# Where an attention kernel divides by its softmax sums: each tile of exponentials on GpSimd, or four query tiles' outputs at once through a float32 product

## The chip, the cores and the metric

The kernel runs on one core of one Trainium2 chip. The metric is the device time of one execution in microseconds (us). A core has a matrix engine (TensorE, PE in the profile; PEld are its weight loads), VectorE (DVE), ScalarE (ACT), GpSimd (POOL) and SyncE (SP), which issues nearly all of this kernel's DMAs. Each engine runs its own queue of instructions in order and waits on semaphores of the others. The kernel uses PSUM, where PE writes its results, as eight banks of 128 x 512 float32.

## The reference, cut to what matters

The model is a two-layer diffusion transformer block on 1024 latent tokens and 256 context tokens, with width 1024. In each layer a modulated norm is followed by a projection and three token mixers side by side (neighbourhood attention, a gated linear scan, a short convolution), an output projection, and a mixture of 16 experts. The change is in the neighbourhood attention. For each of six heads of 64 channels, a query sees 8 rows x 16 columns of latent keys around it, and all 256 context keys:

```python
s_loc = einsum('bjqhd,bjkhd->bhjqk', q_r, k_loc) * scale + bias
s_loc = where(win_mask, s_loc, -inf)
s_ctx = einsum('bjqhd,bchd->bhjqc', q_r, k_ctx) * scale
p = softmax(concatenate([s_loc, s_ctx], -1), -1)
o_loc = einsum('bhjqk,bjkhd->bjqhd', p[..., :n_loc], v_loc)
o_ctx = einsum('bhjqc,bchd->bjqhd', p[..., n_loc:], v_ctx)
return o_loc + o_ctx
```

In the first layer the context tokens also attend to one another; in the second they are not needed.

## The kernel before, in words

Each layer runs norm, projection with scan and convolution, neighbourhood attention, output projection, routing and experts, in this order. The document calls the attention and the part of the output projection beside it the attention stage. It handles the six heads as three pairs (`na_pair`, L771). A pair's queries are cut into tiles of 128, and these into groups: in layer 0 a group of two context tiles, and in both layers two groups of four latent tiles. That makes nine groups in layer 0 and six in layer 1, three of the fifteen with two tiles and twelve with four.

For one tile and one head, `na_scores` (L708) takes the products of queries and keys on PE into two PSUM banks (`sA`, `sB`; the keys are split in a high and a low part, so each is a pair of products). DVE adds the bias, negates and takes the minimum over the row (L743, L745, into `S` and `mn`). ACT takes the exponential in place and sums each row into `sm` (L750). DVE inverts the sum (L751), and POOL multiplies the whole 128 x 832 (768 at the edges, 256 for context) tile by it (L752). `na_transpose` (L755) turns the tile in pieces of 128 x 128 on PE into bank stream "A" (`npt`, two banks taken in turn); ACT and DVE copy them to `PT`. Then PE multiplies them with the values into `nao`, one bank for the whole group, both heads side by side: rows are channels (head 0 in rows 0 to 63, head 1 in 64 to 127), columns are queries. At the group's end ACT copies `nao` to `mo`, and SP stores it to DRAM (`mix`), from where the output projection reads it again (`mst`, L813).

`S`, `PT` and `mo` have two buffers each. Beside the attention runs other work. While pairs 0 and 1 are computed, `na_prep` (L647) makes the next pair's queries and keys (`qn`, `nro`, `qd` on DVE and POOL, transposes `nt` on PE, `QT`, `KH`, `KL`), and `adaln` streams the modulation weights (`wm`) through PE (`aps`). Beside pair 2 runs `wout_part` (L831): the part of the output projection (`po`) that doesn't need the attention. In the tables below, stage one is pairs 0 and 1, stage two is pair 2 with `wout_part`.

The order on each engine is not that of the code: the framework's scheduler places every instruction by its own estimate of times, so a change in one place can move many others. `order` rows below are taken from the built programs.

## Time and profile before

| what | value |
|---|---|
| three timed runs | 2744.39, 2754.39, 2755.64 us, median 2754.39 |
| the profiled execution's own time | 2748.93 us |
| its span in the trace | 2747.2 us |
| stage one, layer 0 and layer 1 | 657 to 784 us, 2066 to 2190 us |
| stage two, layer 0 and layer 1 | 784 to 912 us, 2190 to 2325 us |

Busy time of an engine is the time in which it has at least one instruction running. A matmul's end is modelled, and they are pipelined, so a busy PE is not always PE at its peak. PEclk is the granted clock of TensorE as a share of its higher level (1.00 is 2.4 GHz, 0.5 is 1.2 GHz). A float32 product is two records on PE in this trace, a transpose or a product of the rounded float32 kind (`fp32r`) is one. The chain of waits follows the work that ended last back from the last instruction, and gives each step to the engine or transfer that it waited for.

### The profile page before, as it was taken

Reading aid. Unit: us, or ns where it says so; the run is one execution under the profiler, and the core shown is the slowest. Engines: PE = TensorE matmul, PEld = TensorE weight load, DVE = VectorE, ACT = ScalarE, POOL = GpSimd, SP = SyncE. Lnnn points to the kernel's source line nnn. Section 1 sums busy time; section 2 is a strip of 40 time slices with the busy share of each in tenths; the row PEclk is TensorE's granted clock in tenths of the full one; section 3 lists DMA queues with packets and bytes.
Section 4 is the critical chain, followed back from the end, with each engine's and each line's share of the span. In section 5 each row is a group of like instructions: output and inputs, shape, how many; then the busy total and the mean of one; then the engine's idle time right before and its main releaser. Section 6 shows DMA issues by size and latency. Waiting matters only on the chain.

```text
span 2747.2 us, 55415 instructions
## 1 busy us (share of the span) xinstructions
PE 2520.3 (92%) x21959; PEld 1923.8 (70%) x21959; DVE 1800.3 (66%) x3542; ACT 1132.7 (41%) x1878; POOL 1050.2 (38%) x1125
## 2 busy tenths in 40 slices
PE   7999999988999979999997999999879899589997
PEld 4988877885577855555554988778864677357664
DVE  4247776756777487777754347677767774687874
ACT  4224434324554534444433324344324454445452
POOL 1035454534544733323321035355554442222242
PEclk9999999998999979999998999999989899789999
DMA  7332324246444857888887332323176355779994
GB/s 277 104 105 71 103 72 124 64 140 209 150 141 148 302 190 261 285 271 296 262 279 231 90 109 72 114 76 103 50 208 222 100 164 185 283 269 369 378 376 129
DMA packets 347938, 507.14 MB, mean 185 GB/s; under 512 B 53380, under 2 KB 203072, under 8 KB 346592
## 3 DMA queue, kind: packets, MB, share of 16 engines
q1 hardware_dynamic: 336416, 465.85, 50.1%
q0 software_dynamic: 11264, 37.75, 5.9%
q8 instruction: 173, 2.83, 0.4%
q14 instruction: 85, 0.70, 0.1%
HBM read 410.10 MB, written 94.90 MB: 184 GB/s over the span
## 4 chain that ended last, share of the span: by engine, by line
PE 71%; DVE 15%; DMA 5%; issue 3%; ACT 2%; POOL 2%; SPq 1%; POOLq 0%; DVEq 0%; ACTq 0%
PE pj L277 15%; PE pg L1280 13%; PE pd L1335 8%; PE pj L288 8%; PE po L828 6%; PE nao L786 3%; PE npt L762 2%; PE pgc L1265 2%; DVE Kt L375 2%; PE aps L157 2%; PE hl L341 1%; PE sA L733 1%; DVE Kt L376 1%; DVE kz L355 1%; PE hl L365 1%
## 5 line engine op out<-in xcount | busy, mean ns | idle before, releaser
L1182 DVE TENSOR_TENSOR ewl<-est,ewh 128x2048 fp32r<-128x2048 f32 x126 | 298.3, 2371 | 112.6 <-ACT ewh L1178 108.1
L1178 ACT CAST ewh<-est 128x2048 fp32r<-128x2048 f32 x128 | 243.5, 1906 | 173.6 <-PE pg L1280 122.6
L277 PE MATMUL pj<-hl,whi 128*128 128x320 f32 (+2 forms) x912 | 314.2, 345 | 0.0
L277 PE MATMUL pj<-hh,whi 128*128 128x320 f32 (+2 forms) x912 | 312.5, 343 | 0.7 <-ACT pev L420 0.7
L277 PE MATMUL pj<-hh,wlo 128*128 128x320 f32 (+2 forms) x912 | 312.9, 343 | 0.0
L288 PE MATMUL pj<-whi,hh 128*128 128x256 f32 x960 | 279.8, 292 | 8.8 <-ACT nev L566 8.5
L288 PE MATMUL pj<-whi,hl 128*128 128x256 f32 x960 | 276.4, 291 | 0.9 <-DVE hl L239 0.9
L288 PE MATMUL pj<-wlo,hh 128*128 128x256 f32 x960 | 276.3, 289 | 0.0
L1335 PE MATMUL pd<-est,hidT 128*128 128x512 f32 x512 | 232.2, 596 | 2.1 <-ACT hidT L1302 2.1
L288 PEld LDWEIGHTS pj<-whi,hh 128*128 128x128 f32 x960 | 187.7, 195 | 12.0 <-ACT nev L566 9.3
L288 PEld LDWEIGHTS pj<-wlo,hh 128*128 128x128 f32 x960 | 187.5, 195 | 2.2 <-issue 1.5
L288 PEld LDWEIGHTS pj<-whi,hl 128*128 128x128 f32 x960 | 185.7, 195 | 3.8 <-DVE hl L239 1.5
L377 POOL TENSOR_TENSOR Qt<-Qt,tot 64x320 f32<-64x320 f32 x144 | 128.8, 894 | 150.9 <-PE hl L341 93.5
L277 PEld LDWEIGHTS pj<-hh,whi 128*128 128x128 f32 x912 | 174.8, 192 | 14.4 <-ACT pev L420 1.0
L277 PEld LDWEIGHTS pj<-hl,whi 128*128 128x128 f32 x912 | 174.9, 192 | 14.0 <-issue 1.2
L277 PEld LDWEIGHTS pj<-hh,wlo 128*128 128x128 f32 x912 | 175.0, 192 | 13.7 <-issue 1.4
L752 POOL TENSOR_SCALAR S<-S,sm 128x768 f32<-128x768 f32 (+2 forms) x108 | 112.7, 1045 | 186.3 <-DVE sm L751 153.2
L1335 PEld LDWEIGHTS pd<-est,hidT 128*128 128x128 f32 x512 | 95.2, 189 | 110.7 <-issue 103.3
L265 DVE TENSOR_TENSOR wlo<-wst,whi 128x1024 fp32r<-128x1024 f32 (+1 forms) x72 | 81.6, 1149 | 138.5 <-ACT whi L264 137.7
L1280 PE MATMUL pg<-ewh,xh 128*128 128x512 f32 x512 | 157.0, 425 | 2.9 <-ACT xh L1235 2.8
L1280 PE MATMUL pg<-ewl,xh 128*128 128x512 f32 x512 | 147.6, 404 | 0.0
L375 DVE TENSOR_TENSOR Kt<-Kt,tot 64x320 f32<-64x320 f32 x144 | 96.5, 670 | 76.7 <-POOL tot L380 39.6
(369 smaller groups left out, 5857.5 us busy)
## 6 DMA issues: line engine op xcount, KB each, us to landing
est<-in_w_exp_gate_dram SPq DMA_DIRECT2D x64, 1024.0 KB
est<-in_w_exp_up_dram SPq DMA_DIRECT2D x64, 1024.0 KB
est<-in_w_exp_down_dram SPq DMA_DIRECT2D x64, 1024.0 KB
wm<-in_w_mod_dram SPq DMA_DIRECT2D x80, 512.0 KB
wst<-in_w_in_dram SPq DMA_DIRECT2D x88, 256.0 KB
pna<-nev SPq DMA_DIRECT2D x180, 64.0 KB
wos<-in_w_out_dram SPq DMA_DIRECT2D x42, 256.0 KB
mst<-mix SPq DMA_DIRECT2D x32, 320.0 KB
```

Of the source, the lines that this page charges most:

```text
L265: nc.vector.tensor_tensor(b, c, a, ALU.subtract)
L277: nc.tensor.matmul(ps[:, :cn], sel(a(k)), b[:, k, c0:c0 + cn], start=n == 0, stop=n == 3 * KD - 1)
L288: nc.tensor.matmul(ps[:, :2 * P], b[:, k, t * P:(t + 1) * P], a(k).rearrange("p a n -> p (a n)"), start=n == 0, stop=n == 3 * KD - 1)
L375: nc.vector.tensor_tensor(v(Kt)[lo, :, 0], v(Kt)[lo, :, 0], bc(lo, 1), ALU.mult)
L377: nc.gpsimd.tensor_tensor(v(Qt)[lo, :, 1], v(Qt)[lo, :, 1], bc(lo, 0), ALU.mult)
L752: nc.gpsimd.tensor_scalar(S[:, :w], S[:, :w], sm[:, 1:2], 1.0, ALU.mult, ALU.mult)
L786: nc.tensor.matmul(po[64 * X:64 * X + 64, gi], V[:kn, tt, 64 * X:64 * X + 64], PT[X][:kn, i], start=i == 0, stop=i == len(ch) - 1, tile_po ...
L828: nc.tensor.matmul(ps, a, b, start=n == 0, stop=n == len(ops) - 1)
L1178: nc.scalar.copy(hi, src)
L1182: nc.vector.tensor_tensor(lo[:, :m], src[:, :m], hi[:, :m], ALU.subtract)
L1280: nc.tensor.matmul(acc[gu], a[:, 4 * hf + k], b[:, 512 * k:512 * k + 512], start=n == 0, stop=n == 3 * KD - 1)
L1335: self.downed = nc.tensor.matmul(po[nn], hT[:, 2 * hf + k], st[:, c:c + 512], start=hf == 0 and k == 0, stop=hf == 1 and k == 1)
```

## The change

The exponentials are no longer scaled. The row sums of a group's tiles go into one tile `sm` (`nsm`, 128 queries x 8: head by query tile; a group of two tiles fills the rest with ones). At the group's end DVE inverts it once; PE transposes it into a bank of stream "A" (`nrt`, 8 x 128); DVE spreads it over a block pattern (`nrr`, 8 x 512, zero but for the query tile that a row belongs to; it takes a buffer of `mo`); PE multiplies this with an 8 x 128 matrix of ones and zeros (`heads8`) into the other bank of "A" (`nrb`), a float32 product whose result holds, for each channel and query, the reciprocal that applies; and DVE multiplies `mo` by it before the store. Two small constant tiles are made in each layer.

```diff
--- before.py
+++ after.py
@@ -624,6 +624,15 @@
         self.zb = tp.tile([P, 256], F32, name="zb")
         nc.gpsimd.memset(self.zb, 0.0)
 
+        self.pick = tp.tile([8, 4], F32, name="pick")
+        nc.vector.tensor_tensor(self.pick, self.idf[:8, 0:4], self.idf[:8, 4:8], ALU.add)
+        self.heads8 = tp.tile([8, 2, 64], F32, name="heads8")
+        for X in range(2):
+            h = tp.tile([8, 1], F32, name=f"hd8{X}")
+            nc.vector.tensor_reduce(h, self.idf[:8, 4 * X:4 * X + 4], AX.X, ALU.add)
+            nc.vector.tensor_copy(self.heads8[:, X], h.to_broadcast([8, 64]))
+        self.heads8 = self.heads8.rearrange("p x c -> p (x c)")
+
     def na_bias(self, l, hd, bp):
 
 
@@ -705,7 +714,7 @@
                         nc.vector.tensor_tensor(KL[:, h, c], pf, KH[:, h, c], ALU.subtract)
         return QT, KH, KL
 
-    def na_scores(self, X, qt, ops, EB, np_, banks):
+    def na_scores(self, X, qt, ops, EB, np_, banks, sm):
 
 
         nc = self.nc
@@ -715,7 +724,6 @@
         r0 = 2 * qt
         S = np_.tile([P, 832], F32, name=f"S{X}", bufs=2)
         mn = np_.tile([P, 2], F32, name=f"mn{X}", bufs=2)
-        sm = np_.tile([P, 2], F32, name=f"sm{X}", bufs=2)
         psB = self.bank(banks, [P, 512], F32, "sB")
         if qt < 0:
             for i, Kx in enumerate((KH, KL)):
@@ -747,9 +755,7 @@
             ch = [(kt // P + i, P, P * i) for i in range(4)] + [(0, P, 512), (1, P, 640)]
             if inner:
                 ch.append((kt // P + 4, 64, 768))
-        nc.scalar.activation(S[:, :w], S[:, :w], AF.Exp, scale=-1.0, bias=mn[:, 1:2], accum_out=sm[:, 0:1])
-        nc.vector.reciprocal(sm[:, 1:2], sm[:, 0:1])
-        nc.gpsimd.tensor_scalar(S[:, :w], S[:, :w], sm[:, 1:2], 1.0, ALU.mult, ALU.mult)
+        nc.scalar.activation(S[:, :w], S[:, :w], AF.Exp, scale=-1.0, bias=mn[:, 1:2], accum_out=sm)
         return S, ch
 
     def na_transpose(self, X, S, ch, np_):
@@ -777,8 +783,11 @@
         groups = ([[-2, -1]] if need else []) + [[0, 1, 2, 3], [4, 5, 6, 7]]
         for grp in groups:
             po = self.bank("D", [P, 4, P], F32, "nao")
+            sm = np_.tile([P, 2, 4], F32, name="nsm", bufs=2)
+            if len(grp) < 4:
+                nc.vector.memset(sm, 1.0)
             for gi, qt in enumerate(grp):
-                st = [self.na_scores(X, qt, ops, EB, ns, banks) for X in range(2)]
+                st = [self.na_scores(X, qt, ops, EB, ns, banks, sm[:, X, gi:gi + 1]) for X in range(2)]
                 PT = [self.na_transpose(X, *st[X], np_) for X in range(2)]
                 ch = st[0][1]
                 for i, (tt, kn, c) in enumerate(ch):
@@ -789,6 +798,16 @@
             n = len(grp) * P
             mo = np_.tile([P, 512], F32, name="mo", bufs=2)
             nc.scalar.copy(mo[:, :n], po.rearrange("p c q -> p (c q)")[:, :n])
+
+            nc.vector.reciprocal(sm, sm)
+            pt = self.bank("A", [8, P], F32, "nrt")
+            nc.tensor.transpose(pt, sm.rearrange("p x g -> p (x g)"), self.idf)
+            rt = np_.tile([8, 4, P], F32, name="nrr", tag="mo", bufs=2)
+            nc.vector.tensor_tensor(rt, pt.unsqueeze(1).to_broadcast([8, 4, P]),
+                                    self.pick.unsqueeze(2).to_broadcast([8, 4, P]), ALU.mult)
+            pb = self.bank("A", [P, 512], F32, "nrb")
+            nc.tensor.matmul(pb[:, :n], self.heads8, rt.rearrange("p g q -> p (g q)")[:, :n], start=True, stop=True)
+            nc.vector.tensor_tensor(mo[:, :n], mo[:, :n], pb[:, :n], ALU.mult)
             c0 = CTX + grp[0] * P
             nc.sync.dma_start(self.mix[hp_, :, c0:c0 + n], mo[:, :n])
 
```

The first place is on PE, in layer 0 where pair 0's last group ends and the context group of pair 1 begins. Before, transposes of the next group (`npt`) stand between the last products of this one (`nao`):

```order
L786 MATMUL nao<-PT_8748,nav 64x128
L786 MATMUL nao<-PT_8737,nav 64x128
L762 MATMUL npt<-idf,S_9108 128x128 x2
L786 MATMUL nao<-PT_8748,nav 64x128
L786 MATMUL nao<-PT_8737,nav 64x128
L786 MATMUL nao<-PT_8748,nav 64x128
L762 MATMUL npt<-idf,S_9118 128x128 x2
L735 MATMUL sB<-KH,QT 128x256
L735 MATMUL sB<-KL,QT 128x256
L762 MATMUL npt<-idf,S_9142 128x128 x2
```

In the changed kernel, at the same place on PE:

```order
L795 MATMUL nao<-PT_8717,nav 64x128
L795 MATMUL nao<-PT_8706,nav 64x128
L795 MATMUL nao<-PT_8717,nav 64x128
L804 MATMUL nrt<-idf,nsm 8x128
L743 MATMUL sB<-KH,QT 128x256
L743 MATMUL sB<-KL,QT 128x256
L809 MATMUL nrb<-nrr,heads_8126 128x512
L768 MATMUL npt<-idf,S_9087 128x128 x2
```

The next group's transposes have moved behind `nrb`; between `nrt` and `nrb`, which waits for DVE's `nrr`, stand two products.

The second place is on PE at the end of layer 0's attention (last group of pair 2). Before, the output projection follows the last `nao` at once:

```order
L786 MATMUL nao<-PT_10471,nav 64x128
L786 MATMUL nao<-PT_10482,nav 64x128
L786 MATMUL nao<-PT_10471,nav 64x128
L786 MATMUL nao<-PT_10482,nav 64x128
L828 MATMUL po_11127<-woh_11055,mh 128x512
L828 MATMUL po_11127<-wol_11056,mh 128x512
```

In the changed kernel:

```order
L795 MATMUL nao<-PT_10376,nav 64x128
L804 MATMUL nrt<-idf,nsm 8x128
L795 MATMUL nao<-PT_10387,nav 64x128
L795 MATMUL nao<-PT_10376,nav 64x128
L795 MATMUL nao<-PT_10387,nav 64x128
L809 MATMUL nrb<-nrr,heads_8126 128x512
L847 MATMUL po_11040<-woh_10968,mh 128x512
```

Three short products stand between `nrt` and `nrb` here, and all of the output projection stands behind `nrb`.

The third place is POOL's queue in layer 1's stage one, where the scaling stood between the steps that prepare the next pair (`nro`, `qd`, the bias mask `T`). Before:

```order
L679 TENSOR_TENSOR nro<-qk,sw 128x16x16 x4
L752 TENSOR_SCALAR S_23332<-S_23332,sm_23334 128x832
L688 TENSOR_TENSOR qd<-qn,nrsy 128x1024
L752 TENSOR_SCALAR S_23348<-S_23348,sm_23350 128x832
L752 TENSOR_SCALAR S_23408<-S_23408,sm_23410 128x832
L752 TENSOR_SCALAR S_23424<-S_23424,sm_23426 128x832
L640 MEMSET T 128x256
```

In the changed kernel:

```order
L688 TENSOR_TENSOR nro<-qk,sw 128x16x16 x4
L697 TENSOR_TENSOR qd<-qn,nrsy 128x1024
L160 MEMSET bt 128x512
L688 TENSOR_TENSOR nro<-qk,sw 128x16x16 x4
L697 TENSOR_TENSOR qd<-qn,nrsy 128x1024
L649 MEMSET T 128x256
```

The scalings are gone from the queue, and the preparing steps follow one another.

## Rows read from the trace of the kernel before

**Rows 1.** The page: busy time, share of the span and instructions of each engine.

```profile
PE 2520.3 (92%) x21959; PEld 1923.8 (70%) x21959; DVE 1800.3 (66%) x3542; ACT 1132.7 (41%) x1878; POOL 1050.2 (38%) x1125
```

**Rows 2.** Busy time by stretch (columns: stretch, length, busy us and instructions per engine, PEclk).

```profile
657.00:784.00 127.00, 121.56 (x892) 75.81 (x891) 96.67 (x279) 68.58 (x142) 58.62 (x58) 1.00 0.50 160
784.00:912.00 128.00, 126.30 (x868) 100.44 (x867) 78.38 (x207) 60.66 (x117) 57.07 (x50) 1.00 0.50 155
2066.00:2190.00 124.00, 109.65 (x751) 68.36 (x748) 91.04 (x238) 57.26 (x107) 58.50 (x50) 0.94 0.49 152
2190.00:2325.00 135.00, 133.40 (x894) 106.51 (x895) 82.47 (x216) 60.93 (x110) 45.65 (x40) 0.98 0.54 170
```

**Rows 3.** Chain of waits by line: layer 0 stages one, two; layer 1 one, two.

```profile
by line: PE aps L157 17.0%; PE nao L786 16.3%; PE npt L762 13.2%; PE sA L733 9.1%; PE nt L697 5.3%; issue 5.0%; PE sB L735 4.6%; POOL S L752 4.4%; DMA wg<-mod 3.4%; DMA wm<-in_w_mod_dram 3.1%; DVE S L743 2.6%; ACT S L750 2.0%; DVE qd L688 1
...
by line: PE po L828 42.9%; PE nao L786 17.1%; PE npt L762 13.8%; PE sA L733 7.1%; DMA wos<-in_w_out_dram 4.1%; PE sB L735 3.4%; DMA mst<-mix 2.6%; PE shp L880 2.6%; ACT PT L765 1.6%; ACT S L750 0.8%; issue 0.8%; PE sB L722 0.7%; PE sB L738 
...
by line: PE nao L786 13.8%; PE aps L157 13.6%; PE npt L762 13.1%; PE sA L733 7.1%; DMA wm<-in_w_mod_dram 6.2%; PE nt L697 5.7%; DVE qn L672 4.4%; DMA wos<-in_w_out_dram 4.0%; POOL qd L688 3.5%; PE sB L735 3.4%; DVE qd L688 3.3%; issue 3.2%;
...
by line: PE po L828 39.9%; PE nao L786 14.9%; PE npt L762 11.3%; PE sA L733 7.7%; issue 4.1%; DMA E<-rpbx 3.6%; PE sB L735 2.8%; DMA wos<-in_w_out_dram 2.0%; POOL E L639 1.6%; DMA part<-wx 1.5%; PE shp L880 1.3%; DVE wol L804 1.0%; DVE S L7
```

**Rows 4.** L752, L762 (layer 1): busy us, mean ns, idle before; or min/median/max ns.

```profile
L752 POOL TENSOR_SCALAR S<-S,sm 128x768 f32<-128x768 f32 (+2 forms) x108 | 112.7, 1045 | 186.3 <-DVE sm L751 153.2
...
L752 POOL TENSOR_SCALAR S<-S,sm x108: 471/962/2054, 661.2 to 2309.7; 128x768 f32<-128x768 f32 x48, 128x832 f32<-128x832 f32 x48, 128x256 f32<-128x256 f32 x12
...
L762 PE MATMUL npt<-idf,S 128*128 128x128 f32 (+1 forms) x312 | 50.1, 291 | 5.0 <-POOL S L752 3.8 <-DVE PT L765 1.2
```

**Rows 5.** Prices on PE: a float32 product's group, and instructions in time order.

```profile
L1335 PE MATMUL pd<-est,hidT 128*128 128x512 f32 x512 | 232.2, 596 | 2.1 <-ACT hidT L1302 2.1
...
801.13 0.40 PE L828 MATMUL po<-woh,mh 128*128 128x512 f32 x1
801.36 0.39 PE L828 MATMUL po<-wol,mh 128*128 128x512 f32 x1
...
2300.63 0.98 PE L762 MATMUL npt<-idf,S 128*128 128x128 f32 x7
2301.37 0.48 PE L733 MATMUL sA<-KH,QT 128*128 128x512 f32 x1
```

**Rows 6.** Prices on DVE, min/median/max ns by line.

```profile
L751 DVE RECIPROCAL sm<-sm x108: 137/160/165, 660.9 to 2309.5; 128x1 f32<-128x1 f32 x108
...
L854 DVE TENSOR_TENSOR wy<-po,wg x16: 675/692/694, 792.6 to 899.4; 128x512 f32<-128x512 f32 x16
```

**Rows 7.** DVE's L672 in ns as above; DVE and POOL around 2147 us.

```profile
L672 DVE TENSOR_TENSOR qn<-qk,cw x18: 683/1226/3081, 600.5 to 2146.7; 128x1024 f32<-128x1024 f32 x12, 128x512 f32<-128x512 f32 x6
...
2146.70 3.08 DVE L672 TENSOR_TENSOR qn<-qk,cw 128x1024 f32<-128x1024 f32 x1 [1.40 <-POOL qd L688]
...
2146.62 2.07 POOL L639 TENSOR_TENSOR E<-E,cm 128x896 f32<-128x896 f32 x1
2148.68 1.88 POOL L752 TENSOR_SCALAR S<-S,sm 128x768 f32<-128x768 f32 x1
```

**Rows 8.** Chain of waits in time order, layer 1 stage one, its POOL pieces.

```profile
2137.49 2.82 POOL nro L679 x4
2140.31 0.90 POOL S L752
```

**Rows 9.** TensorE's clock: one stretch of 50 us, and transposes at both levels.

```profile
2150.00:2200.00 50.00, 42.24 (x287) 33.39 (x288) 37.31 (x91) 25.41 (x48) 21.94 (x16) 0.83 0.38 119
...
2141.25 1.54 PE L762 MATMUL npt<-idf,S 128*128 128x128 f32 x6 [0.24 <-POOL S L752]
...
2310.44 0.85 PE L762 MATMUL npt<-idf,S 128*128 128x128 f32 x6 [0.61 <-DVE PT L765]
```

**Rows 10.** SP's queue at the end of layer 0's attention.

```profile
912.37 0.32 SPq L793 DMA_DIRECT2D mix<-mo  x1
...
920.57 0.91 SPq L813 DMA_DIRECT2D mst<-mix  x2
```

## The prediction

> **What bounds the kernel now.** First the page's list of engines: PE is busy 92% of the span, the next one, DVE, 66%, and POOL, from which the change takes work, only 38% [rows 1]. An average over stages says little, so next the table of stretches for the four parts in which the changed lines run. In both stages two PE is the bound: 126.3 of 128 us in layer 0, 133.4 of 135 in layer 1. In stages one it is busy 121.6 of 127 and 109.7 of 124 us, and the clock's mean in layer 1 is 0.94 [rows 2]. Then the chain of waits of each stretch [rows 3], for what the end hangs on: in stage one of layer 0 the six PE lines make 65.5% (17.0 + 16.3 + 13.2 + 9.1 + 5.3 + 4.6), in layer 1 56.7% (13.8 + 13.6 + 13.1 + 7.1 + 5.7 + 3.4). The step that goes, POOL's L752, is 4.4% of 127 us = 5.6 us in layer 0's stage one, and is not among the lines listed in either stage two, where the smallest one listed for layer 0 has 0.7%. So 112.7 us of POOL's work [rows 4] stand almost wholly beside the path. After the attention come output projection, routing and experts in a row, so I let what the stages lose or win pass on whole.
>
> The sum is made against the profiled execution, 2748.93 us (span 2747.2). The three timed runs are 2744.39, 2754.39 and 2755.64 us: it lies between them, 5.5 us under their median.
>
> **PE: two added products for each of 15 groups.** `nrt` is a transpose: seven of them issue in 2301.37 - 2300.63 = 0.74 us, 0.11 us each [rows 5]. `nrb` is a float32 product of 512 columns. The trace has it as `pd`: 512 records, two to a product, 232.2 us busy, so 2 x 0.4535 = 0.91 us [rows 5]; with 256 columns half, 0.45. That it has 8 rows instead of 128 to sum over I count as no saving. Bounds: from below the rounded kind's 0.23 us (801.36 - 801.13), from above two records that don't overlap, 2 x 0.596 = 1.19 us [rows 5]. I take 0.91, since it is the same kind and width. A group of four tiles costs 1.02 us, one of two 0.56.
>
> - Stages two: 2 x 1.02 + 0.56 = 2.6 in layer 0, 2.04 in layer 1. PE is full there, so all of it counts: +4.6 us.
> - Stages one: 4 x 1.02 + 2 x 0.56 = 5.2 in layer 0, 4.08 in layer 1. I count PE's share of the chain: 0.655 x 5.2 + 0.567 x 4.08 = 3.4 + 2.3 = +5.7 us.
>
> Lower end of both: 0.34 us for a four-tile group in stages two (0.23 for the context one), nothing in stages one, 1.6 us. Upper end: all on the path at 1.30 and 0.71, 12 x 1.30 + 3 x 0.71 = 17.7 us.
>
> **A new wait on PE.** `nrb` waits for DVE's `nrr`, which waits for `nrt`: the transpose's 0.28 us (291 ns mean [rows 4]), the spread on DVE 0.69 (512 elements per row out of PSUM, as L854 [rows 6]), and two hand-overs at 0.04 (POOL's 2140.31 + 0.90 to PE's 2141.25 [rows 8, 9]) make 1.05 us. What PE has between `nrt` and `nrb` covers it where there is enough. By the built program's order the rows between number 11, 15, 3, 12, 5, 16, 40, 25, 4 in layer 0 and 12, 9, 14, 13, 29, 4 in layer 1. Four of 15 have five or fewer, with some 0.25 us of work; there PE stands 0.8 us, and behind it the next group's transposes or, at both layers' ends, the output projection: 4 x 0.8 = +3.2 us. Bounds: 0 if DVE's turn comes at once and the scheduler's next products are early, 15 x 1.05 = 16 us if none is covered.
>
> **What goes.** On the chain: 5.6 us of L752 in layer 0 [rows 3]. In layer 1 one piece, 0.90 us, but it had stood in POOL's queue behind the four `nro` steps (2.82 us, [rows 8]), which then hold no transposes up: 3.7 us. Together -9.3 us. From below: 3.8 us, if only what PE itself is shown waiting for in layer 1 goes [rows 4] and ScalarE's exponential is as late otherwise; from above, the clock as well (below). In stages two I count nothing, as nothing listed waits for it.
>
> **DVE.** 108 reciprocals go, 108 x 0.16 = 17.3 us [rows 6]. Added: 12 x (0.16 + 0.69 + 0.69) = 18.5, for the three small groups a fill more, at most a reciprocal's time, 3 x 1.70 = 5.1, and ten small instructions for the constants at up to 0.16, 1.6: +7.9 us net. DVE is busy 96.7 of 127, 78.4 of 128, 91.0 of 124 and 82.5 of 135 us [rows 2]: PE's work covers it, 0; without cover it costs 7.9. ACT's work stays.
>
> **The stores.** The last group's store issues at 912.37 us, and the read-back behind it at 920.57 [rows 10]: 8.2 us of room for the 2.4 that the new tail adds (0.8 + 0.91 + 0.69). Hidden.
>
> **POOL and DVE on one port.** At 2146.62 us POOL began a step of 2.07 us; DVE's `qn`, begun at 2146.70, took 3.08 us where its median is 1.23, and L752, begun at 2148.68, took 1.88 where its median is 0.96 [rows 4, 7]: each ran after the other, and here L752 was the one that lost. Over all 108, its mean is 83 ns above its median, 9 us. The Trainium skill (SBUF — State Buffer, Who interferes with whom) has the pair's shared port as a lock: an instruction of VectorE with two SBUF inputs and one of GpSimd that reads SBUF don't overlap, and whichever began first keeps it. By that rule VectorE should have lost about as much to L752, some 9 us as an estimate, and had all of it been on the path the sum below would come to 2744. The trace agrees on the lock; the one case looked at has VectorE waiting for another GpSimd step. For the sum I take what rows 7 show, 0.
>
> **The sum.** 2748.93 + 4.6 + 5.7 + 3.2 - 9.3 = 2753.1 us. Forecast: 2753 us, with its own range of 2743 to 2764.
>
> **Rivals.**
>
> *Hidden altogether* (0.15). PE stands by in stage one, and the added products fall into its waits; only stages two pay: 2748.9 + 4.6 - 9.3 = 2744 us. For it: 14 us without PE busy in layer 1's stage one [rows 2]. Against it: 5 us in layer 0's.
>
> *POOL's queue paces stage one* (0.21). With no scaling in it, the next pair's preparation and the tiles both run ahead, the stalls at `nrb` vanish, and TensorE keeps its clock. In layer 1, 2150 to 2200 us, it was granted 0.83: six transposes took 1.54 us after a wait for L752, against 0.85 at full clock [rows 9]. Stage one's mean of 0.94 over 124 us stands for 7.4 us. Then 2748.9 + 4.6 - 9.3 - 7.4 = 2737 us. For it: POOL's order changes most there, `nro` and `qd` follow one another. Against it: POOL is busy under half of stage one [rows 2].
>
> *The group's end becomes a serial section* (0.22), the one on the other side. `nrt` and `nrb` take both banks of stream "A", and these come free only when DVE has multiplied `mo`: 0.28 + 0.69 + 0.91 + 0.28 + 0.69 + 5 x 0.04 = 3.05 us in which the next group's transposes, which before stood between the last products of the old one, can't run. If the other work doesn't fill that in stages one, with ten groups, it costs 10 x 3.05 = 30 us: 2748.9 + 30 + 4.6 - 9.3 = 2774 us. It decides from the point where PE waits over 1 us a group before L768 for DVE's last product. For it: the transposes have moved behind `nrb` in the order. Against it: products of scores and the preparation's transposes stand there too, and stages two have `po`.
>
> **How the numbers follow.** The forecast's own case has 0.42. What a measurement of this kernel can tell from no change is about 0.5%, so 2740.6 and 2768.2 us around the median. The rival with POOL ends mostly below, "hidden" now and then: faster 0.2. The serial section ends mostly above, and the forecast with the upper price of its products at times: slower 0.21. The rest, 0.59, is the same. The scheduler also reorders instructions behind the stages, in layer 0's experts, whose work is the same; I count 0, and the range has room for it. It reaches from 2737, the rival with POOL, to 2774, the serial section.
>
> **What would show it.** Right: stages two longer by about 2.6 and 2.0 us, with `nrb` at about 0.9 us; stages one within 3 us of 127 and 124; PE idle before L809 for DVE's L806 in some four places. Wrong: stage one shorter by 6 us or more with the clock at 1.00, or PE's idle before L768 and L809 above 15 us, or a change of more than 5 us in layer 0's experts.

## The result, and the profile after

The changed kernel takes 2786.29 us (median of four runs, 2784.80 to 2788.53) against 2749.96 us for the kernel before beside it: a ratio of 1.0139, 95% interval 1.0122 to 1.0156. I had forecast no change, 2753 us, with a range up to 2774. The profiled execution spans 2784.1 us, 36.9 more than before's.

The page's engines after, the row that answers to [rows 1]:

```profile
PE 2559.0 (92%) x22004; PEld 1925.7 (69%) x22004; DVE 1799.3 (65%) x3492; ACT 1133.5 (41%) x1878; POOL 918.7 (33%) x1017
```

POOL is relieved of 131 us, as meant; PE is busy for 39 us more, though the added products are 45 records. The stretches after (columns as in [rows 2]): layer 0's stages one and two, layer 1's stages one and two, and layer 0's experts once they run evenly.

```profile
658.00:790.00 132.00, 129.16 (x902) 76.72 (x900) 95.34 (x258) 66.72 (x139) 26.98 (x24) 0.99 0.49 150
790.00:928.00 138.00, 137.01 (x883) 104.63 (x884) 80.07 (x203) 65.11 (x124) 35.30 (x26) 0.98 0.54 167
2099.00:2222.00 123.00, 112.71 (x800) 70.17 (x801) 93.69 (x229) 58.20 (x111) 30.41 (x28) 0.97 0.50 156
2222.00:2360.00 138.00, 134.90 (x847) 100.93 (x847) 81.00 (x195) 59.09 (x106) 19.88 (x15) 0.97 0.49 156
1110.00:1486.00 376.00, 375.79 (x1924) 190.53 (x1922) 253.13 (x325) 151.15 (x156) 97.29 (x75) 1.00 0.83 272
```

The four stages are longer by 5, 10, -1 and 3 us: 17 of 37. The last row says where to look for the rest: layer 0's experts, which the change doesn't touch, with PE full and at full clock. Read along the timeline, with names that come up from here on (`lgk`: the routing's products, the first behind the output projection; in an expert, `pg`: the products that go up, `hidp`: four transposes of its hidden layer, once per expert, `pd`: the products that go down), the loss against before is 0.8 us at attention's start, 15.4 at layer 0's last copy of `mo`, 19.3 at the first `lgk`, 16.8 at the first `pg`, 22.9 at the third expert's `hidp`, 32.5 at the last expert's, and 37.0 at layer 1's last `hidp`. Layer 0 holds nearly all of it.

Part of one expert before and after, on PE (start, duration, line, operation, shapes, count). Before:

```profile
1181.36 1.06 PE L1265 MATMUL pgc<-est,xct 128*32 128x512 f32 x8
1183.25 1.92 PE L1341 MATMUL pdc<-est,hcT 128*32 128x512 f32 x16
1187.79 1.07 PE L1265 MATMUL pgc<-est,xct 128*32 128x512 f32 x8
1195.80 4.45 PE L1335 MATMUL pd<-est,hidT 128*128 128x512 f32 x10
1200.18 1.92 PE L1265 MATMUL pgc<-est,xct 128*32 128x512 f32 x16
1202.04 2.84 PE L1335 MATMUL pd<-est,hidT 128*128 128x512 f32 x6
1205.27 0.64 PE L1300 MATMUL hidp<-idf,hid 128*128 128x128 f32 x4
```

After, out of one expert, with the same products:

```profile
1209.58 1.06 PE L1284 MATMUL pgc<-est,xct 128*32 128x512 f32 x8
1214.84 1.06 PE L1284 MATMUL pgc<-est,xct 128*32 128x512 f32 x8
1221.28 1.06 PE L1284 MATMUL pgc<-est,xct 128*32 128x512 f32 x8
1222.28 0.74 PE L1299 MATMUL pg<-ewh,xo 128*128 128x512 f32 x2
1222.85 1.08 PE L1299 MATMUL pg<-ewl,xh 128*128 128x512 f32 x4
1223.86 1.06 PE L1284 MATMUL pgc<-est,xct 128*32 128x512 f32 x8
1224.86 3.70 PE L1354 MATMUL pd<-est,hidT 128*128 128x512 f32 x8
1228.49 1.07 PE L1360 MATMUL pdc<-est,hcT 128*32 128x512 f32 x8
1229.48 3.70 PE L1354 MATMUL pd<-est,hidT 128*128 128x512 f32 x8
1233.12 1.06 PE L1360 MATMUL pdc<-est,hcT 128*32 128x512 f32 x8
1234.33 0.64 PE L1319 MATMUL hidp<-idf,hid 128*128 128x128 f32 x4
```

The context products `pgc` and `pdc` (32 columns wide, four beside each other on PE) stand in four stretches per expert before and in six after. From `hidp` to `hidp` an expert takes 27.23 us before and 28.08 after, over seven periods each.

What the page says of the changed step itself, PE's lines that answer to [rows 4], here for both layers, and the new product's (idle before, and what ended it):

```profile
L768 PE MATMUL npt<-idf,S 128*128 128x128 f32 (+1 forms) x648 | 103.5, 286 | 3.2 <-ACT PT L771 1.6 <-DVE PT L771 1.5
L809 PE MATMUL nrb<-nrr,heads 8*128 8x512 f32 (+1 forms) x30 | 16.5, 629 | 1.2 <-DVE nrr L806 1.2
```

The transposes no longer wait for POOL, and PE's marked waits at the new product come to 1.2 us. What the attention lost is in no wait that carries the new tiles' names; that made the experiments necessary. In layer 0 it is in no other wait of PE either. From layer 0's first score product to its first `lgk` (columns as in [rows 2]), before and after:

```profile
636.98:919.04 282.06, 266.95 (x1835) 188.83 (x1835) 195.75 (x514) 141.52 (x279) 133.97 (x123) 0.97 0.55 173
637.83:938.32 300.49, 286.92 (x1872) 196.08 (x1873) 196.68 (x485) 145.49 (x286) 84.81 (x66) 0.95 0.56 170
```

The stretch is 18.4 us longer with 1.5 us less of PE idle. Added up from start to start over the two traces' records, `nrt` and `nrb` make 9.5 us of it. Seven more products of `po` ahead of the first `lgk` make some 1.6. The rest, close to 9 us, is in products that both kernels have (`nao` 2.8, `aps` 2.5, `po` 2): the same work takes PE longer, in another order and at a granted clock of 0.95 on the mean where it was 0.97 (in 780 to 800 us 0.83: PE stands 1.1 us between 788 and 792 and is granted 0.50 from 792 to 796; before, though it stands 1.6 us in these 20, has 1.00). How much of the 9 is the order and how much the clock, no run separates.

### The profile page after: what moved, and what is told of

It is laid out like the page before. It is cut to its first block, busy times and chain, and to the rows that moved or that the text cites. A ratio compares the mean times of both kernels' runs of the same rounds, so it can differ in the third digit from the quotient of the medians.

```text
span 2784.1 us, 55190 instructions
## 1 busy us (share of the span) xinstructions
PE 2559.0 (92%) x22004; PEld 1925.7 (69%) x22004; DVE 1799.3 (65%) x3492; ACT 1133.5 (41%) x1878; POOL 918.7 (33%) x1017
## 4 chain that ended last, share of the span: by engine, by line
PE 57%; DVE 8%; DMA 5%; issue 4%; POOL 2%; ACT 1%; SPq 1%; POOLq 0%; ACTq 0%; DVEq 0%
PE pg L1299 13%; PE pd L1354 8%; PE pj L277 6%; PE po L847 5%; PE pj L288 5%; PE nao L795 3%; PE pgc L1284 2%; PE npt L768 2%; PE aps L157 2%; PE sA L741 1%; PE xt L1250 1%; PE pdc L1360 1%; DVE Kt L375 1%; DVE Kt L376 1%; DVE kz L355 1%
## 5 line engine op out<-in xcount | busy, mean ns | idle before, releaser
L277 PEld LDWEIGHTS pj<-hl,whi 128*128 128x128 f32 x912 | 174.0, 191 | 13.5 <-issue 1.2
L1299 PE MATMUL pg<-ewh,xo 128*128 128x512 f32 x512 | 145.2, 399 | 1.5 <-DVE xo L1255 1.5
```

The source lines that it names most:

```text
L277: nc.tensor.matmul(ps[:, :cn], sel(a(k)), b[:, k, c0:c0 + cn], start=n == 0, stop=n == 3 * KD - 1)
L1299: nc.tensor.matmul(acc[gu], a[:, 4 * hf + k], b[:, 512 * k:512 * k + 512], start=n == 0, stop=n == 3 * KD - 1)
```

## The experiments

All runs, each against the kernel before beside it on the same chip. The last column is (ratio - 1) x 2750 us. Names with a_ are variants of the changed kernel, with b_ of the one before.

| run | median us | ratio, 95% interval | us against before |
|---|---|---|---|
| changed kernel | 2786.3 | 1.0139 (1.0122, 1.0156) | +38 |
| a_late_hct | 2771.7 | 1.0087 (1.0073, 1.0100) | +24 |
| b_late_hct | 2742.8 | 0.9981 (0.9972, 0.9989) | -5 |
| b_one_transpose | 2772.2 | 1.0090 (1.0077, 1.0103) | +25 |
| a_no_product | 2743.8 | 0.9989 (0.9980, 0.9997) | -3 |
| a_add_only | 2759.1 | 1.0047 (1.0029, 1.0064) | +13 |
| a_product_no_wait | 2761.9 | 1.0054 (1.0036, 1.0073) | +15 |
| a_rounded_nrb | 2769.4 | 1.0074 (1.0060, 1.0087) | +20 |
| a_bank_of_po | 2776.1 | 1.0098 (1.0083, 1.0113) | +27 |
| a_store_on_act | 2768.6 | 1.0080 (1.0066, 1.0093) | +22 |
| a_end_delayed | 2780.6 | 1.0117 (1.0095, 1.0139) | +32 |
| a_plan_held | 2786.4 | 1.0139 (1.0123, 1.0154) | +38 |
| a_paired_context | 2770.6 | 1.0089 (1.0074, 1.0103) | +24 |
| b_transpose_first | 2746.5 | 0.9995 (0.9987, 1.0004) | -1 |
| b_scale_each | 2750.8 | 1.0019 (1.0010, 1.0028) | +5 |
| b_transpose_each | 2772.7 | 1.0093 (1.0077, 1.0109) | +26 |
| b_plan_held | 2749.6 | 1.0010 (1.0001, 1.0019) | +3 |
| b_context_last | 2741.4 | 0.9974 (0.9963, 0.9984) | -7 |
| b_paired_context | 2737.3 | 0.9964 (0.9952, 0.9975) | -10 |

### Is it the experts' order?

a_late_hct and b_late_hct: one edit of the experts' code, in either kernel.

```diff
 def expert_hid(self, l, r, up, ep):
...
-            ps = self.bank("downc", [P, 2, 64], F32, "hct")
...
 def expert_down(self, l, r, hid, ep, g5, g5c, xl, xc):
...
-            for k in range(2):
-                if need:
+        if need:
+            ps = self.bank("downc", [P, 2, 64], F32, "hct")
...
+        for hf in range(2):
+            st = r["down"][hf]
+            for k in range(2):
+                if need:
```

> The changed kernel with one edit in layer 0's experts: the transposes hct and the context products pdc are emitted behind the products pd, which gives PE the same repeating order per expert that the kernel before has (hidp 4, pg 12, pgc 4, pg 3, pdc 8, ... pd 5, pgc 8, pd 3, hct 2); attention and everything else stay as changed. Theory 'order': about 0.8 us per expert and the start-up, some 12 to 16 of the 36 us lost, come from the order in which the scheduler put PE's instructions there; the time is 2770 to 2775 us, ratio to before 1.007 to 1.010, period from hidp to hidp 27.25 us. Rival 'attention alone': the experts are slower because of what the changed attention does to them (memory, clock, late loads), so the period stays 28.05 us and the time 2784 to 2789 us, ratio 1.013 to 1.015.

> The kernel before with the same edit of the experts' code: its repeating order stays as it was, and the order of PE in layer 0's attention is the same row by row. Both theories: within 3 us of before, 2747 to 2753 us, ratio 0.999 to 1.001. If the edit itself gained or lost more, the run a_late_hct has to be read against this one and not against before.

In both kernels the code now has `hct` and `pdc` (the context tokens' transposes and products) behind both halves of `pd`. The period in a_late_hct is 27.23 us, and it is 14 us faster than the changed kernel. The edit itself gains 5 us on the kernel before, 2 more than expected: from the thirteenth expert's `hidp` to the last `pdc` the experts take 3.3 us less (before has five and seven stretches of context products in two of these last experts, b_late_hct four). So the attention's part is 24 + 5 = 29 us, and the experts' order has the rest.

b_one_transpose: ahead of layer 0's output projection.

```diff
+            if l == 0 and hp_ == 2 and grp[0] == 4:
+                pz = self.bank("A", [P, 4, P], F32, "dum")
+                for i in range(1):
+                    nc.tensor.transpose(pz[:, i % 4], V[:, i % 10], self.idf)
+                self.bank("A", [P, 4, P], F32, "dum")
```

> The kernel before with one needless 128x128 transpose (about 0.11 us of PE) ahead of layer 0's output projection; attention's own order in layer 0 is unchanged, but the scheduler then gives layer 0's experts the order that the changed kernel has (pgc and pdc in pieces of four). Theory 'order': period 28.05 us per expert, 12 to 16 us more than before, 2762 to 2766 us, ratio 1.0045 to 1.006, with no change of over 2 us up to the end of layer 0's output projection. Rival 'attention alone': 2750 us, ratio 1.000, period 27.25 us.

The theory's direction held, its size was too small: +25 us from 0.11 us of work. The period is 28.08 us; the loss is 3.8 us at the last copy of `mo`, 7.9 at the first `lgk` (2 at most were expected up to there), 19.6 at the third expert's `hidp` and 28.2 at the thirteenth's. The start of the experts loses more than the period's 0.85 us explains. PE's waits there, for the routing's transposes `ctp`, the experts' token transposes `xt` and `pg`, 1000 to 1100 us of this kernel (us in total, times, longest):

```profile
PE ctp L1086 <- DVE ctb L1084: 11.2, 2, 8.5
PE xt L1236 <- DVE xm L1238: 3.6, 2, 3.1
PE pg L1285 <- ACT xh L1240: 3.1, 1, 3.1
```

Of the kernel before, in the same stretch:

```profile
PE ctp L1081 <- DVE ctb L1079: 8.3, 1, 8.3
...
PE xt L1231 <- DVE xm L1233: 0.8, 1, 0.8
PE pg L1280 <- ACT xh L1235: 0.8, 1, 0.8
```

The three waits come to 17.9 us against 9.9: the first experts' transposes and products stand where DVE's and ScalarE's part of the start isn't done.

b_context_last (the first pair of lines; `expert_ctx` holds the context half taken out of `expert_hid`) and b_paired_context (the other lines, on b_late_hct): fewer stretches of context products.

```diff
-                self.expert_down(l, rs[e], hid, ep, g5, g5c, xl, xc)
+                self.expert_down(l, rs[e], (hid, self.expert_ctx(l, sc, ep)), ep, g5, g5c, xl, xc)
...
-                    if len(late) > 1 * first:
-                        ctx_mm(*late.pop(0))
+                    if hf and not first:
+                        ctx_mm(*late.pop(0))
+                        ctx_mm(*late.pop(0))
...
```

> The kernel before with the context half of each expert's hidden layer (hcp, its Silu, hct) emitted behind the next expert's products pg: attention unchanged, and PE's order in layer 0's experts has still fewer pieces (557 stretches of one kind against 594 before, 664 in the changed kernel). If a switch between kinds of products costs PE time, as before against b_one_transpose suggests (70 stretches more, 0.85 us a period), the period falls by some 0.4 us to 26.8 us and the time by 6 us, 2739 to 2744 us. If it is the number of short context pieces alone that counts, which is pgc 4 + 8 or 8 + 8 in both: 27.2 us and 2743 to 2749 us. If the later chain makes PE wait for the context half: above 2752 us.

> b_late_hct with the context products pgc of both halves of a weight matrix issued together (one stretch of 16 instead of two of 8), so that an expert has three stretches of column-tiled products (pgc, pgc, pdc) where before has four and the changed kernel six. Between before and b_one_transpose two stretches more cost 0.85 us a period, 0.42 each. If that price holds: period 26.8 us and 16 x 0.42 = 6.7 us less than b_late_hct's 2742.8, 2733 to 2739 us, ratio to before 0.994 to 0.997. Rival 'the price belongs to the changed order of pd and pg and not to the number of stretches': period 27.2 us, 2740 to 2746 us.

b_paired_context has a period of 26.90 us and is the fastest kernel of all, 0.36% under before. Three, four and six stretches give 26.90, 27.23 and 28.08 us: 0.33 and 0.42 us a stretch. The 0.33 is the cleaner price: between four and six, other products (`hct`, `xt`) have moved too. b_context_last also has three, but a period of 28.49 on the mean (26.5 to 30.8 from expert to expert): the period that was expected failed, though the time, 2741.4 us, lies where it was expected. Its later chain makes PE wait (1170 to 1460 us), where the others' PE is full:

```profile
PE xtc L1244 <- DVE val L1160: 3.9, 3, 1.4
PE hidp L1300 <- DVE hid L1297: 2.0, 2, 1.2
```

The waits, 5.9 us, are about half of what its seven periods have over 26.90. The profiled run is the slowest of its eleven, 2747.84 us, as slow as before. The median is 7 us below before's; whether the faster runs have these waits, no trace shows.

### What does the end of a group cost?

a_no_product, a_add_only and a_product_no_wait are steps of one ladder, all on a_late_hct. The first leaves out these lines:

```diff
-            nc.vector.reciprocal(sm, sm)
-            pt = self.bank("A", [8, P], F32, "nrt")
...
-            nc.vector.tensor_tensor(mo[:, :n], mo[:, :n], pb[:, :n], ALU.mult)
```

> The changed kernel with the edit of a_late_hct, and without everything at a group's end but the copy and the store: no reciprocals, nrt, nrr, nrb and no multiplication of mo, so the division by the sums is left out of the output. It prices apart what goes (108 reciprocals and POOL's scalings) and what comes. Theory 'the products are paid in full and nothing is gained': this kernel takes as long as b_late_hct, 2747 to 2753 us, and a_late_hct is some 20 us above it. The prediction's own steps (9.3 us gained by what goes) would give 2738 to 2743 us, and the products 13.5 us above that. Rival 'the exponentials left unscaled cost by themselves' (the finer order of PE): 2756 us or more.

The second has in their place

```diff
+            nc.vector.reciprocal(sm, sm)
+            nc.vector.tensor_tensor(m3, m3, self.zb.unsqueeze(1).to_broadcast([P, n // 256, 256]), ALU.add)
```

with `m3` a view of `mo` and `zb` a tile of zeros, and the third

```diff
+            pb = self.bank("A", [P, 512], F32, "nrb")
+            nc.tensor.matmul(pb[:, :n].rearrange("p (g q) -> p g q", q=P), self.heads8,
+                             self.heads8.unsqueeze(1).to_broadcast([8, len(grp), P]), start=True, stop=True)
+            nc.vector.tensor_tensor(mo[:, :n], mo[:, :n], pb[:, :n], ALU.mult)
+            self.turn["A"] += 1
```

behind the same reciprocals (the last line keeps the turn of the two banks). All three leave the division by the sums out of the output.

> a_late_hct without nrt, nrr and nrb; at a group's end DVE takes the reciprocals and adds a constant tile to mo in place of the multiplication, before the store (the division by the sums is left out). It prices DVE's step and the later store alone. Theory 'the cost comes from PE's products and the chain nrt, nrr, nrb': within 3 us of a_no_product's 2743.8, so 2741 to 2748 us. Rival 'the later store holds the queue or the read-back': 2755 us or more.

> a_late_hct with nrb kept at its size and place but fed by a constant, so that it waits for neither nrt nor nrr (both are gone; the division by the sums is left out). PE pays 12 x 0.91 + 3 x 0.45 = 12.3 us and DVE still multiplies by the product. PE's order then has about as few pieces as before (316 and 273 stretches against 360 and 303 in the changed kernel). Theory 'PE's time': 2752 to 2758 us, 8 to 14 us above a_no_product, and the chain the other 14 to 20 us below a_late_hct's 2771.7. Rival 'the chain and the order alone': within 3 us of a_no_product, 2741 to 2747 us. Rival 'the held bank': 2766 us or more.

What goes gains nothing: a_no_product is 2 us slower than b_late_hct (their intervals overlap), not 9.3 faster. Its attention in layer 1 does end 16.9 us earlier than b_late_hct's, by the last copy of `mo`, but the first `lgk` behind the output projection comes only 3.0 earlier: in between, PE has 57 products of `po` left where b_late_hct has 42, and stands 7.5 us. By layer 1's last `hidp` it is 2.6 us behind. What comes costs 27 us, twice the 13.5 predicted, in steps of 16, 2 and 9. The 2 is within the noise, and a_product_no_wait, 2761.9 us, lies outside all three ranges expected of it, nearest to that of PE's time. The first step, with no product on PE at all, is the largest; there my theory fell, and the rival with the read-back has the time right. In its trace the time is lost where attention hands over to the output projection of layer 0 (20.5 us from the last copy of `mo` to the first `lgk`, 8.2 in a_no_product):

```profile
912.90 1.52 PE L795 MATMUL nao<-PT,nav 128*64 128x128 f32 x22
919.51 0.79 PE L841 MATMUL po<-woh,mh 128*128 128x512 f32 x1 [5.09 <-ACT mh L827]
920.10 0.63 PE L841 MATMUL po<-wol,mh 128*128 128x512 f32 x1
```

PE has no product ready there and waits 5.1 us for the read-back of `mix`; behind that stand 54 products of `po` ahead of the first `lgk`, where a_no_product has 33. How many are left is set by the scheduler's order.

a_rounded_nrb, a_bank_of_po, a_store_on_act and a_end_delayed each change one thing in a_late_hct: `nrr` (and `heads8`) in the rounded kind, the bank of `nrt` and `nrb`, the store's queue, and the place of the end, which `finish` holds.

```diff
+            rt = np_.tile([8, 4, P], F32R, name="nrr", tag="mo", bufs=2)
...
+            pb = self.bank("D", [P, 512], F32, "nrb")
...
+            nc.scalar.dma_start(self.mix[hp_, :, c0:c0 + n], mo[:, :n])
...
+                if gi == 0 and pend:
+                    finish(*pend)
```

> a_late_hct with the product nrb in the rounded kind (one record of 0.23 us for 512 columns instead of two of 0.45; the reciprocals are rounded). Theory 'PE's time is paid in full': 12 x 0.68 + 3 x 0.33 = 9.2 us less than a_late_hct's 2771.7, so 2760 to 2765 us, ratio to before 1.005 to 1.0065. Rival 'the order and the serial end, not the product itself': within 3 us of a_late_hct, 2769 to 2775 us, since the wait on DVE's nrr and the held banks stay.

> a_late_hct with nrt and nrb in the bank of the accumulated outputs (stream D), which the copy has just emptied, instead of the two banks A that the transposes npt use; the next group's transposes need not wait for the multiplication of mo, and PE's order in layer 0's attention has about as few pieces as before (306 stretches of one kind against 315 before and 360 in the changed kernel). Theory 'held banks and the finer order cost some 7 us in layer 0 and as much in layer 1 at most': 2757 to 2766 us, ratio 1.0035 to 1.0068. Rival 'only PE's time counts': 2769 to 2775 us. If the wait moves to the next group's first product into the same bank: 2775 us or more.

> a_late_hct with the store of mo issued from ScalarE's queue instead of SP's, so that loads behind it on SP (mst, wx) don't wait for the multiplication of mo. PE's order is unchanged. Rival 'SP's queue is held': stages two lose their waits, 4 to 8 us less than a_late_hct, 2763 to 2768 us. Theory 'order and PE's time': 2769 to 2775 us, ratio 1.0075 to 1.010.

> a_late_hct with a group's end (reciprocals, nrt, nrr, nrb, multiplication, store) emitted behind the first tile of the next group, so that PE has that tile's products between; the last group of a pair as before. All the work stays. Theory 'the chain at the group's end makes PE wait': 9 of 15 ends are covered, so half or more of some 14 us comes back, 2758 to 2765 us. Rival 'it is PE's time and the finer order of its pieces' (369 and 307 stretches, more than in a_late_hct): 2768 to 2776 us.

With the rounded product `nrb` is busy 7.8 us instead of 15.5, but the kernel is only 2 to 4 us faster than a_late_hct, with overlapping intervals; the rival's range was right. Its profiled run is the slowest of six, 2776.3 us against a median of 2769.4. In it the copies of `mo` run ahead of a_late_hct's by 2.4 us at layer 0's fourth, and by 0.6 at the last. Its clock, in two stretches in which it fell back (columns as in [rows 2]):

```profile
740.00:760.00 20.00, 17.19 (x105) 11.86 (x106) 14.10 (x35) 10.65 (x28) 6.04 (x3) 0.83 0.35 77
920.00:930.00 10.00, 7.62 (x36) 5.70 (x37) 2.40 (x4) 3.24 (x6) 4.30 (x6) 0.66 0.36 129
```

a_late_hct has a clock of 1.00 in both, with 18.02 and 9.81 us busy (between 780 and 800 us it is the slower one, 0.83 against 0.91). In this run PE spent what it saved standing or at the lower clock; for the faster ones no trace shows it. The bank of `po` is no better (2776.1 us), though PE's order has fewer pieces: their number alone doesn't tell the time in attention. That time was expected if the wait moved to the next group's first product, but the trace marks no such wait. The store's queue is at most a small part: a_store_on_act, 2768.6 us, lies between the two ranges expected of it, and its interval and a_late_hct's overlap for the most part. Delaying the end doesn't help: 2780.6 us, above both ranges.

### Is it the work or the plan?

b_transpose_first, b_transpose_each and b_scale_each add nearly nothing to b_late_hct, at the place of the change's products (the first added line is b_scale_each, the others are the transposes).

```diff
+            nc.vector.tensor_scalar(mo[:, :n], mo[:, :n], 1.0, None, ALU.mult)
             nc.sync.dma_start(self.mix[hp_, :, c0:c0 + n], mo[:, :n])
+            pz = self.bank("A", [P, 4, P], F32, "dum")
+            nc.tensor.transpose(pz[:, 0], V[:, 0], self.idf)
+            self.bank("A", [P, 4, P], F32, "dum2")
```

> b_late_hct with one needless 128x128 transpose (0.11 us) behind one group of layer 0's first pair. Theory 'a new plan costs by itself': some place differs from b_late_hct by 3 us or more without its work, in either direction, and the time is outside 2740 to 2746 us. Rival 'only the work counts': 2740 to 2746 us.

> b_late_hct with one needless 128x128 transpose behind each of the 15 groups' stores: 15 x 0.11 = 1.7 us of PE, nothing waits for it; the experts' repeating order stays. Theory 'a new plan costs by itself' (any instruction at the groups' ends makes the scheduler lay attention and what follows anew): 2750 to 2760 us, 7 us or more above b_late_hct's 2742.8. Rival 'only the work counts': 2743 to 2747 us.

> b_late_hct with DVE multiplying mo by 1.0 at each group's end, before the store; POOL's scalings stay. a_add_only, the same step without POOL's scalings, took 15 us more than a_no_product, of which 12 lie between the last copy of mo and the first lgk of layer 0. Theory 'the later last store and the plan made for it': 2752 to 2760 us, and that stretch is longer than before's 8.2 us by 4 us or more. Rival 'what a_add_only lost belongs to that plan alone': within 3 us of b_late_hct, 2740 to 2746 us.

One transpose in one group gives 2746.5 us, half a microsecond outside the bounds of "only the work counts": inconclusive. Fifteen of them, 1.7 us of PE, cost 31 us above b_late_hct, 13 above the range expected of a new plan. More than half of it is lost by the first `lgk` of layer 0, as in a_late_hct (15.4 us, of 24.5 at the end of the profiled run, which is 6.5 us below the median). DVE's scaling costs 10 us above b_late_hct, which puts it between the two ranges, and not in the hand-over (9.9 us, expected 12 or more): between the first `lgk` and the first expert's `hidp` the loss goes from 4.4 to 18.1 us, and 8.4 of that come back by layer 1's last `hidp`.

b_plan_held is b_transpose_each, and a_plan_held a_bank_of_po, with each instruction of an engine chained, without a wait, behind the one that comes before it in a given plan: for b_plan_held b_late_hct's on all engines, for a_plan_held a_no_product's on PE and ScalarE.

```diff
+                    tc.add_manual_dep(ins[at], last.name,
+                                      mybir.DependencyInfo(mybir.DependencyClass.NoSync, mybir.DependencyReason.DATA),
+                                      reason="plan")
+                last = ins[at]
```

> b_transpose_each once more, with the same 15 needless transposes, but every engine's instructions are chained in the order that the scheduler had made for b_late_hct; only the 15 transposes are added to it, on PE. Theory 'a new plan costs by itself': the 30 us of b_transpose_each are gone and 1.7 us or less are left, 2741 to 2748 us. Rival 'the transposes' use of the two banks A or of PE costs it': 2765 us or more, as b_transpose_each's 2772.7.

> a_bank_of_po once more, the same work with nrt and nrb in the bank of the outputs, but PE's and ScalarE's instructions are chained in the order of a_no_product; nrt stands 9 and nrb up to 24 instructions behind a group's last product, both ahead of the next group's first. DVE, POOL and the queues are planned anew. Theory 'most of what the attention loses is the new plan, and the work costs PE's time': 2743.8 + 12.3 + 1.7 and up to 6 us of waits where the next group's products follow closely, 2754 to 2764 us against a_bank_of_po's 2776.1. Rival 'the work and its chain cost it, whatever the plan': 2771 to 2781 us.

With the plan of b_late_hct kept, 23 of the 31 us that the transposes had cost are gone (2749.6 us, 1.6 above what was expected). This shows that a plan made anew can cost that much by itself. The change is another matter: with a_no_product's order on PE kept, the same work as in a_bank_of_po takes 10 us more (2786.4 against 2776.1, above the rival's range as well), and the theory that most of the loss is the plan fell there. PE's waits in its layer 0, 634 to 942 us:

```profile
PE nt L706 <- POOL qd L697: 5.9, 2, 5.0
PE nt L706 <- DVE QT L711: 4.8, 6, 1.5
PE nao L795 <- DVE mo L810: 3.8, 5, 1.0
PE nrb L809 <- DVE nrr L806: 3.5, 3, 2.2
```

and in a_late_hct's, 634 to 937 us, where the scheduler laid PE's work around the chain:

```profile
PE nt L706 <- POOL qd L697: 6.0, 2, 5.1
PE nt L706 <- DVE QT L711: 3.2, 5, 0.9
PE sB L730 <- DVE KL L714: 1.3, 1, 1.3
PE nrb L809 <- DVE nrr L806: 1.0, 3, 0.5
```

Held in the old order, the chain `nrt`, `nrr`, `nrb`, `mo` is the serial section that I had as a rival, 7.3 us of waits in layer 0. In the free plan these waits are mostly gone, and the time is paid in PE's busy time. (a_plan_held leaves DVE, POOL and the queues free, and has the products in another bank, so it is no exact copy.)

a_paired_context: the experts' edit that helped most, in the changed kernel.

> The changed kernel with the edits of b_paired_context in the experts. If the price of a stretch of column-tiled products is independent of the attention: as far below a_late_hct's 2771.7 as b_paired_context lies below b_late_hct (5.5 us), 2763 to 2769 us, period 26.9 us. If the experts' gain is lost again behind them: 2770 to 2775 us.

Its one edit more is the second of the experts' diffs above. The period is 26.90 us, as expected, and the profiled run, the fastest of five at 2764.3 us, ends 9 us before a_late_hct's. But the median, 2770.6 us, is only 1 us lower, in the range for a gain that is lost again, and the intervals overlap: whether the experts' gain reaches the end here stays open.

## Why the prediction was wrong

The 38 us are 14 (the experts' edit, by which a_late_hct is faster) + 27 (what comes at a group's end) + 2 (what goes, not clear of the noise) - 5 (what the same edit gains on the kernel before). The experts' order alone is thus 9 to 14 here (in b_one_transpose, with a worse start, it is most of 25). The rows for the products' price, on PE, and for the last store, on DVE and SP's queue, all of the changed kernel:

```profile
787.22 1.12 PE L809 MATMUL nrb<-nrr,heads 8*128 8x512 f32 x2
788.27 0.66 PE L768 MATMUL npt<-idf,S 128*128 128x128 f32 x4
```

```profile
927.00 0.69 DVE L810 TENSOR_TENSOR mo<-mo,nrb 128x512 f32<-128x512 f32 x1 [1.28 <-PE nrb L809]
```

```profile
927.72 0.32 SPq L812 DMA_DIRECT2D mix<-mo  x1
```

- *"The scheduler also reorders instructions behind the stages, in layer 0's experts, whose work is the same; I count 0"*: this step failed first. Same work in six stretches in place of four costs 0.85 us an expert, with PE full before and after, and a worse start besides. The sign I named for it, over 5 us in layer 0's experts, appeared. The built order of the experts has these pieces in plain sight; the prediction used it for the attention alone.
- *"What goes: -9.3"*: failed, +2. A share of the chain is what stood last there, not what is won when it goes. The rival "POOL's queue paces stage one" was wrong too: layer 1's stage one, with a clock of 0.97, is 1 us shorter and not 7.4, and in layer 0 `nt` still waits 6.0 us for POOL's `qd`, 5.2 before. Of the 9 us in the paragraph on the port most came, and the time didn't follow: VectorE's five steps of the attention stage with two inputs from SBUF (`qd`, both `qn`, `wol`, `ml`) take 126.5 us before and 118.4 after.
- *The products, +4.6 and +5.7*: their price was nearly right. Two records of `nrb` take PE 1.05 us from start to next start (787.22 to 788.27), where 0.91 was estimated from `pd` [rows 5]. They take 0.53 and 0.52 us, where a `pd` in the middle of its stretch takes 0.43: a product that stands by itself pays at both ends. `nrt` and `nrb` of layer 0's nine groups occupy 9.5 us from their starts to the next, besides 1.0 of waiting ahead of `nrb`, and 6 x 1.02 + 3 x 0.56 = 7.8 were estimated. Weighting them with PE's share of the chain was wrong: PE's idle time hardly shrank, so in layer 0 they stand in its busy time in full. Nor are they a term that can be bought back: a_rounded_nrb, where 9.2 us of PE were expected to go, gains 2 to 4. And the sum had nothing for the same products taking longer, close to 9 us in layer 0.
- *The wait at `nrb`, +3.2*: 1.2 us marked in the profile. (The rows counted between `nrt` and `nrb` are one too many: the two places printed above have two and three, not three and four.) Too high as a wait, far too low as the price of the chain: a_late_hct stands 9 us above a_product_no_wait, which has the product without the chain, though in another order.
- *DVE's +7.9 us hidden, the stores hidden*: not safe. a_add_only, DVE's step and the later store alone, costs 16; with POOL's scalings kept (b_scale_each) the step costs 10, lost at another place, so part of it belongs to the order. In the changed kernel the last copy of `mo` to the first `lgk` takes 12.1 us where before takes 8.2; the store issues at 927.72, behind the multiplication of 927.00, where [rows 10] has 912.37.
- *The serial section*, 2774 us, came nearest among the rivals in number, by luck: its chain exists (a_plan_held), but the changed kernel doesn't show it where I said to look. PE idles 3.2 + 1.2 us before L768 and L809, not 15.
- Of the signs for "right", only `nrb`'s price and the stages of layer 1 came near (-1 and +3 us); layer 0's stages are 5 and 10 us longer.

What stays open is how the 27 us divide between the chain and the plan. A plan alone can cost 23 us (b_transpose_each against b_plan_held). But the old order, held, is 10 us worse for the new work than the scheduler's own (a_plan_held against a_bank_of_po). No run has the changed kernel's work, in its own banks, in an order as good for it as the old one is for the old work.

## What to carry to other kernels

Where a scheduler lays out the whole program anew, price the new order and not the edit alone: compare the built orders in every later stage that runs with PE full, above all the number of stretches of narrow products. Test a price with a needless edit of the same size at the same place, and with the order held: if the needless edit costs as much, the sum of instruction prices says little. A step off the critical path that is taken away gains what the next one leaves, here nothing.

## What the runs showed of the hardware

A stretch more of the context products (32 columns, four beside each other), with the same number of products, costs PE 0.33 to 0.42 us. Eight records take 0.99 us from start to next start (1228.49 to 1229.48), sixteen in one stretch 1.85 (1183.25 to 1185.10), and the products on either side of a stretch lose the rest. By the single records, the last `pd` ahead of a stretch takes 0.52 us to the next start and the first one behind it 0.53, where 0.43 is usual; the last `pdc` of the stretch takes 0.52 as well. The Trainium skill (TensorEngine Tiling (Array Packing), Key Properties) says that a change of the tiling mode drains TensorE. These runs fit that, and put a price on it, of which a part is not the mode's own: the first `pg` behind the plain transposes `hidp` also takes 0.32 us where 0.23 is usual. The granted clock fell where PE had stood: in a_rounded_nrb PE was busy 0.39 us from 920 to 922, and in the next four steps of 2 us it was granted 0.52, 0.50, 0.50 and 0.77, where 0.50 is the lower level, 1.2 GHz; a_late_hct, with 9.81 us busy in 920 to 930, kept 1.00.
